# Matmul, GELU, matmul on one core: nine of the first twelve loads cast inside the transfer, and two banks for one turn

## The chip, the core and the metric

The kernel runs on one core of one Trainium2 chip. The metric is the device time of a run in microseconds (us), the median of three runs: 118.3 us for the kernel before (118.18 to 118.35). The profile is of one execution and spans 116.2 us from the first to the last instruction; TensorE's granted clock was 0.999 in it.

## The reference

```python
m, k, n, p = 1024, 1024, 2048, 1024          # a: m x k, b: k x n, c: n x p, all float32
h = np.matmul(a, b)
h = 0.5 * h * (1 + np.tanh(np.sqrt(2 / np.pi) * (h + 0.044715 * h ** 3)))
return np.matmul(h, c).astype(np.float32)
```

## The kernel before

The inputs lie in memory as float32. The kernel works with bf16 operands and with float32 sums of bf16 blocks, and its order is written out by hand: on each engine the instructions run in the order of the code.

**What is loaded, and how.** `a` is needed transposed. Its 1024 rows are cut into an upper and a lower half (h = 0, 1), its 1024 columns into four parts (q = 0 to 3) of 256. The first 512 columns of `b` are loaded by q too, two row tiles of 128 at a time. For each q there are three loads of 512 KB in float32: a's upper part, b's part, a's lower part. All twelve go on SyncE's queue (`load_a`, line 70, and `load_b`, line 74) into staging tiles `sta` and `stb`, still float32. The rest of `b` and the whole of `c`, fourteen transfers, go on GpSimd's queue (lines 89 to 95); those transfers cast to bf16 on the way, so each reads 1 MB and writes 512 KB. A copy of one column, `gate` (line 84), stands ahead of them on GpSimd: it waits for the load of a's lower part of q = 2, and so holds GpSimd's queue back.

A framework puts the waits in. On each of the two queues it uses eight completion counters in turn, so a transfer's issue waits until the one eight places ahead of it has landed.

**The first stage** (lines 214 to 294). For each part of `a`, `cast_a` casts the staged part to bf16 tiles `ab`, on VectorE (line 101) or ScalarE (line 99), or one half on each. `turn` (line 127) transposes it: in two halves (n = 0, 1), four transposes on TensorE into a PSUM bank (line 132) and a copy from the bank into `aT` by VectorE (line 133). `cast_b` casts b's rows on ScalarE (line 139). `block` issues matmuls that accumulate the products of the first row tiles of the hidden matrix (line 105), each 128x512 with 128 deep. The turns are split by `next(tn)`, so that matmuls stand between the two halves of a turn: a turn has one bank for both halves, and the second half's transposes wait for the copy of the first. `stir` (line 116) keeps TensorE at work before data is there. `zero.t1` and others (line 155) prepare sums of blocks on VectorE for the next stage.

One bank number matters for the change: the first turn of a's lower half, `turn(1, 0, 7, ab)` at line 225, uses bank 7, with two matmuls between its halves. Bank 6 is to hold `ps[1, 2]`, an accumulator that starts just after.

**The rest.** Three times a product of 2x2 blocks is computed with seven products instead of eight (class `Seven`, function `seven`, matmuls at line 197): `zero` and `one` for the rest of the hidden matrix, with b's other columns, and `two` for the second matmul with `c`. Each result tile of `two` is stored by SyncE (line 436), most as one transfer of 128x512.

Of the kernel before, what the change touches and what calls it, by code (L numbers as in the profile page):

```python
# [9 lines left out]
F32 = mybir.dt.float32  # L10
F32R = mybir.dt.float32r
BF16 = mybir.dt.bfloat16
# [7 lines left out]
def kernel(ctx, tc, a, b, c, out):  # L20
    nc = tc.nc
    M, K = a.shape
    _, N = b.shape
    _, P = c.shape
    H = 512
# [3 lines left out]
    av = a.rearrange("(mt p) k -> p mt k", p=128)  # L29
    bv = b.rearrange("(kt p) n -> p kt n", p=128)  # L30
# [9 lines left out]
    def slot(tag, shape, dt, name):  # L40
        return big.tile(shape, dt, name=name, tag=tag)

    def bank(i, shape=(128, H), dt=F32, name="ps"):
        return pp.tile(list(shape), dt, name=name, tag=f"bank{i}", padded_shape=None)

    def pieces(tag, bufs, shape, dt, name):
        return small.tile(shape, dt, name=name, tag=tag, bufs=bufs)
# [5 lines left out]
    gate = consts.tile([128, 1], F32, name="gate")  # L53
# [7 lines left out]
    b1 = slot("b1", [128, KT, 1024], BF16, "b1")  # L61
# [2 lines left out]

    KH = KT // 2
    stb = slot("x0", [128, KT, H], F32, "stb")
    sta = [slot(f"x{i}", [128, 2, 2, 4, 256], F32, "sta") for i in (1, 3)]

    def load_a(h, q):
        nc.sync.dma_start(out=sta[q // 2][:, h, q % 2],  # L70
                          in_=av[:, 4 * h:4 * h + 4, ds(q * 256, 256)])

    def load_b(q):
        nc.sync.dma_start(out=stb[:, 2 * q:2 * q + 2], in_=bv[:, 2 * q:2 * q + 2, 0:H])

    load_a(0, 0)
    load_b(0)
    load_a(1, 0)
    for q in range(1, 4):
        load_a(0, q)  # L80
        load_b(q)
        load_a(1, q)

    nc.gpsimd.tensor_copy(gate, sta[1][:, 1, 0, 3, 0:1])
    nc.scalar.activation(g, warm[:, 0:1], AF.Gelu_apprx_tanh)


    for k in range(0, KT, 4):
        nc.gpsimd.dma_start(out=b1[:, k:k + 4, H:], in_=bv[:, k:k + 4, ds(H, H)])
    for n in range(2):  # L90
        for k in range(0, KT, 4):
            nc.gpsimd.dma_start(out=b2[:, k:k + 4, ts(n, H)],
                                in_=bv[:, k:k + 4, ds(1024 + n * H, H)])
# [3 lines left out]
    def copy(eng, dst, src):  # L97
        if eng is nc.scalar:
            nc.scalar.activation(dst, src, AF.Copy)  # L99
        else:  # L100
            nc.vector.tensor_copy(dst, src)  # L101

    def mm1(p, t, h, ks):
        for k in ks:
            nc.tensor.matmul(p, b1[:, k, ts(t, 128)], aT[:, h, k],  # L105
                             start=(k == 0), stop=(k == KT - 1))
# [6 lines left out]
    def stir(*widths):  # L113

        for w in widths:
            nc.tensor.matmul(ps[0, 3][:, 0:w], warm[:, 0:128], warm[:, 0:w],  # L116
                             start=True, stop=True, skip_group_check=True)

    def cast_a(h, q, *engs):

        ab = pieces("ab", 2, [128, 4, 256], BF16, "ab")
        for i, eng in enumerate(engs):
            w = 256 // len(engs)
            copy(eng, ab[:, :, ts(i, w)], sta[q // 2][:, h, q % 2][:, :, ts(i, w)])
        return ab

    def turn(h, q, i, ab):

        pt = bank(i, (128, 2, H), BF16, "pt")
        for n in range(2):  # L130
            for m in range(4):
                nc.tensor.transpose(pt[:, n, ts(m, 128)], ab[:, m, ts(n, 128)], ident)  # L132
            nc.vector.tensor_copy(aT[:, h, 2 * q + n], pt[:, n])  # L133
            yield

    def cast_b(k, n=1):
        for i in range(n):
            r = ds(i * (H // n), H // n)
            nc.scalar.activation(b1[:, k, r], stb[:, k, r], AF.Copy)  # L139

    def block(h, tiles, ks):
        for k in ks:
            for t in tiles:
                mm1(ps[h, t], t, h, (k,))
# [62 lines left out]
    def quarters(b, c0, w):  # L207
        return [[b[:, 0:4, ds(c0, w)], b[:, 4:8, ds(c0, w)]],
                [b[:, 0:4, ds(c0 + w, w)], b[:, 4:8, ds(c0 + w, w)]]]

    zero = Seven(4, quarters(b1, H, 256), BB, [None] * 4, [None] * 4, 2)
    one = Seven(4, quarters(b2, 0, H), BB, [None] * 4, zero.t)

    stir(256, 256, 256, 256)
    tn = turn(0, 0, 4, cast_a(0, 0, nc.vector))
    next(tn)
    stir(256)
    next(tn)
    stir(128)
    cast_b(0, 2)  # L220
    cast_b(1)
    ab = cast_a(1, 0, nc.vector, nc.scalar)
    block(0, range(4), (0,))
    block(0, range(2), (1,))
    tn = turn(1, 0, 7, ab)
    next(tn)
    block(0, range(2, 4), (1,))
    next(tn)
    for t in range(3):
        ps[1, t] = bank(4 + t)  # L230
    zero.t[0], zero.t[1] = pair(2)
    zero.t1(4, 0)
    ab = cast_a(0, 1, nc.scalar, nc.scalar)
    block(1, range(3), (0,))
    tn = turn(0, 1, 7, ab)
    next(tn)
    block(1, range(3), (1,))
    next(tn)
    cast_b(2)
    cast_b(3)  # L240
    ab = cast_a(1, 1, nc.vector, nc.scalar)
    block(0, range(4), (2,))
    block(0, range(1), (3,))
    tn = turn(1, 1, 7, ab)
    next(tn)
    block(0, range(1, 4), (3,))
    next(tn)
    zero.t1(4, 1)
    ab = cast_a(0, 2, nc.scalar, nc.scalar)
    block(1, range(3), (2,))  # L250
    tn = turn(0, 2, 7, ab)
    next(tn)
    block(1, range(3), (3,))
    next(tn)
    cast_b(4)
    cast_b(5)
    ab = cast_a(1, 2, nc.vector, nc.scalar)
    block(0, range(4), (4,))
    block(0, range(1), (5,))
    tn = turn(1, 2, 7, ab)  # L260
    next(tn)
    block(0, range(1, 4), (5,))
    next(tn)
    zero.t1(4, 2)
    ab = cast_a(0, 3, nc.scalar, nc.scalar)
    block(1, range(3), (4,))
    tn = turn(0, 3, 7, ab)
    next(tn)
    block(1, range(3), (5,))
    next(tn)  # L270
    zero.t1(4, 3)
    cast_b(6)
    cast_b(7)
    ab = cast_a(1, 3, nc.scalar, nc.vector)
    block(0, range(4), (6, 7))
    zero.t2(2, 0)
    for t in range(4):
        gelu(t, 0, ps[0, t])
    ps[1, 3] = bank(7)
    mm1(ps[1, 3], 3, 1, range(2))  # L280
    tn = turn(1, 3, 0, ab)
    next(tn)
    mm1(ps[1, 3], 3, 1, range(2, 5))
    next(tn)
# [150 lines left out]
    def store(mt, q0, w, ot, eng=None):  # L435
        (eng or nc.sync).dma_start(out=out[ts(mt, 128), ds(q0, w)], in_=ot)

    def done2(i, l, j, p):
        if (i, l) == (1, 0):
            ot = pieces("o", 4, [128, H], F32, "ot")  # L440
            nc.vector.tensor_copy(ot, p)
            p = ot
        n = 2 if (i, l) == (0, 0) else 1
        for q in range(n):
            r = ds(q * (H // n), H // n)
            store(4 * i + j, l * H + q * (H // n), H // n, p[:, r])

    def between2(n):
# [12 lines left out]
        elif n == "P73":  # L461
            two.t4(two.t[1], 4)

    seven(two, done2, between2)


# [28 lines left out]
```

## Time and profile before

| | us |
|---|---|
| time, median of 3 | 118.3 |
| span of the profile | 116.2 |
| TensorE busy in the span | 111.7 |
| VectorE, ScalarE, GpSimd busy | 90.3, 59.3, 11.0 |
| from the first transposes (line 132) to the first matmul of line 197, by the chain | 4.99 to 24.95 |
| the 400 matmuls of line 197, by the chain | 88.03 |

How to read the profile: PE is TensorE's matmul side, PEld its weight load, DVE is VectorE, ACT ScalarE, POOL GpSimd, SP SyncE; POOLq and SPq are those engines' own instruction queues. A row of the timeline is the start, the duration, the engine, the line, the operation and its tiles, and in brackets how long the engine had been idle and what ended that. Ends of matmuls are modelled: a matmul of 512 columns is shown as 379 ns although the next one starts after 216, so starts are to be compared and not busy times. "The chain of waits" follows the execution back from its last instruction, at each step to what released it; each of its rows is a start, a length and what the time went to. Of the transfers the profile gives packets and bytes by queue: q1 holds SyncE's, q0 GpSimd's. The bytes of casting transfers are counted as they are written, in bf16, so 206 GB/s there means 412 GB/s read.

While the first stage runs, the transfers move 390 GB/s or so from 7 us on (391 between 10 and 13 us), and 298 between 2.9 and 5.8 us.

### The profile page before, as it was taken

The page shows a single profiled execution, that of the slowest core. Times are in us where ns is not written, and L with a number is a line of the kernel's source. Part 1 is how long each engine was busy: PE and PEld are TensorE (multiplying, and loading weights), DVE is VectorE, ACT ScalarE, POOL GpSimd, SP SyncE. Part 2 cuts the span into 40 slices and gives each one's busy share as a digit, 9 for nine tenths or more (in the row PEclk, how much of TensorE's full clock was granted, in tenths as well). Part 3 has the DMA queues.
Part 4 walks back from the last instruction along what each step waited for, and adds up shares of the span by engine and source line. Part 5 has one row for each costly group of instructions (what it writes and reads, how often), then busy time and mean ns, then how long its engine had stood idle before and what let it go on. Part 6 is the DMA issues. An engine that isn't in the chain of part 4 may idle for free.

```text
span 116.2 us, 1478 instructions
## 1 busy us (share of the span) xinstructions
PE 111.7 (96%) x540; PEld 76.9 (66%) x540; DVE 90.3 (78%) x107; ACT 59.3 (51%) x99; POOL 11.0 (9%) x21
## 2 busy tenths in 40 slices
PE   5999999999999999999999999999999999999980
PEld 4655555545777447888885444588888888888860
DVE  0336666889998999844699999999999986954770
ACT  5067668989269998066699329600034982000000
POOL 2000049623322000000000000000000000000000
PEclk9999999999999999999999999999999999999999
DMA  2999999999999999998000000070000002014993
GB/s 83 298 356 393 395 395 321 206 206 206 206 208 213 211 213 211 213 209 164 4 0 0 0 6 0 7 264 0 0 0 0 0 0 96 0 69 171 370 364 109
DMA packets 13542, 17.91 MB, mean 154 GB/s; under 512 B 736, under 2 KB 8928, under 8 KB 13536
## 3 DMA queue, kind: packets, MB, share of 16 engines
q0 software_dynamic: 5344, 7.34, 35.6%
q1 hardware_dynamic: 8192, 10.49, 25.2%
q8 instruction: 4, 0.07, 0.2%
q14 instruction: 2, 0.02, 0.0%
HBM read 20.97 MB, written 4.19 MB: 217 GB/s over the span
## 4 chain that ended last, share of the span: by engine, by line
PE 96%; DVE 1%; issue 0%
PE ps L197 76%; PE ps L105 12%; PE ps L116 4%; PE pt L132 4%; DVE aT L133 0%; DVE ot L382 0%; DVE warm L50 0%
## 5 line engine op out<-in xcount | busy, mean ns | idle before, releaser
L197 PE MATMUL ps<-x,s 128*128 128x512 f32 x128 | 29.6, 391 | 0.0
L197 PEld LDWEIGHTS ps<-x,s 128*128 128x128 f32 x128 | 24.0, 188 | 5.1
L197 PE MATMUL ps<-x,x 128*128 128x512 f32 x96 | 22.9, 394 | 0.0
L197 PEld LDWEIGHTS ps<-x,x 128*128 128x128 f32 x96 | 18.0, 188 | 3.9
L105 PE MATMUL ps<-aT,b 128*128 128x512 bf16 x64 | 16.3, 379 | 0.0
L305 ACT ACTIVATE v<-ps 128x512 f32<-128x512 f32 x10 | 6.0, 598 | 19.4 <-PE ps L197 19.4
L197 PE MATMUL ps<-c_sb,hT 128*128 128x512 bf16 (+1 forms) x72 | 14.2, 356 | 0.0
L197 PE MATMUL ps<-x 128*128 128x512 f32 x56 | 13.2, 393 | 0.0
L197 PEld LDWEIGHTS ps<-x 128*128 128x128 f32 x56 | 10.2, 188 | 2.7 <-ACT u L305 0.4
L133 DVE COPY aT<-pt 128x512 bf16<-128x512 bf16 x16 | 6.8, 424 | 6.4 <-PE pt L132 6.4
L197 PEld LDWEIGHTS <-hT 128*128 128x128 bf16 x72 | 6.9, 98 | 7.0 <-issue 0.5
L109 ACT ACTIVATE hT<-ot 128x512 bf16<-128x512 f32 x18 | 10.5, 625 | 1.5 <-DVE ot L310 1.3
L310 DVE TENSOR_TENSOR ot<-ps,v 128x512 f32<-128x512 f32 x10 | 6.7, 688 | 5.2 <-DMA out_dram<-ot 3.8
L197 PE MATMUL ps<-aT,b 128*128 128x512 bf16 x48 | 10.7, 379 | 0.0
L310 DVE TENSOR_TENSOR ot<-ps,u 128x512 f32<-128x512 f32 x10 | 6.7, 689 | 5.1 <-ACT u L305 5.1
L155 DVE TENSOR_TENSOR x<-c_sb 128x1024 fp32r<-128x1024 bf16 x8 | 9.2, 1221 | 0.0
L132 PEld LDWEIGHTS <-ab 128*128 128x128 bf16 x64 | 4.9, 102 | 5.5 <-DVE ab L101 1.9
L197 PEld LDWEIGHTS <-b 128*128 128x128 bf16 x48 | 4.6, 97 | 5.7 <-issue 0.3
L105 PEld LDWEIGHTS <-b 128*128 128x128 bf16 x64 | 5.5, 98 | 4.1 <-ACT b L139 0.5
L99 ACT ACTIVATE ab<-sta 128x512 bf16<-128x512 f32 x10 | 6.0, 625 | 3.3 <-DMA sta<-in_a_dram 3.3
L305 ACT ACTIVATE u<-ps 128x512 f32<-128x512 f32 x10 | 5.8, 596 | 3.4 <-PE ps L197 3.2
L109 ACT ACTIVATE hT<-ps 128x512 bf16<-128x512 f32 x14 | 7.3, 596 | 0.4 <-PE ps L105 0.3
(39 smaller groups left out, 115.6 us busy)
## 6 DMA issues: line engine op xcount, KB each, us to landing
sta<-in_a_dram SPq DMA_DIRECT2D x8, 512.0 KB, 8.4
c_sb<-in_c_dram POOLq DMA_DIRECT2D x8, 512.0 KB, 19.9
b<-in_b_dram POOLq DMA_DIRECT2D x6, 512.0 KB, 11.5
out_dram<-ot SPq DMA_DIRECT2D x12, 256.0 KB, 2.1
stb<-in_b_dram SPq DMA_DIRECT2D x4, 512.0 KB, 8.0
out_dram<-ot SPq DMA_DIRECT2D x8, 128.0 KB, 2.0
```

The costliest lines, as they stand in the source:

```text
L99: nc.scalar.activation(dst, src, AF.Copy)
L105: nc.tensor.matmul(p, b1[:, k, ts(t, 128)], aT[:, h, k], start=(k == 0), stop=(k == KT - 1))
L109: nc.scalar.activation(hT[h][:, t], p, AF.Gelu_apprx_tanh)
L116: nc.tensor.matmul(ps[0, 3][:, 0:w], warm[:, 0:128], warm[:, 0:w], start=True, stop=True, skip_group_check=True)
L132: nc.tensor.transpose(pt[:, n, ts(m, 128)], ab[:, m, ts(n, 128)], ident)
L133: nc.vector.tensor_copy(aT[:, h, 2 * q + n], pt[:, n])
L155: nc.vector.tensor_tensor(out=dst[:, r], in0=x[:, r], in1=y[:, r], op=op)
L197: nc.tensor.matmul(p[:, ds(c0, w)], l[:, k, ts(j, 128)], r[:, k, ds(c0, w)], start=(start and k == 0), stop=(k == self.kt - 1), skip_group ...
L305: nc.scalar.activation(st, p, AF.Copy)
L310: nc.vector.tensor_tensor(out=ot, in0=p, in1=st, op=ADD)
```

## The change

Only the first three loads stay on SyncE's queue: a's upper part, b's part and a's lower part of q = 0. The other nine go on GpSimd's queue, ahead of what it had, and are cast to bf16 inside the transfer: a's parts into a new tile `abq`, b's parts right into `b1`. So their casts on ScalarE and VectorE, and their waits for them, fall away. The copy `gate` that opens GpSimd's queue now waits for a's first load instead of its lower part of q = 2. With the staging no longer needed, the code for q = 1 and 2 becomes a loop; the order of the matmuls and turns in it is kept.

The first turn of a's lower half gets two banks, 7 and 6, one for each half, so that its eight transposes follow each other; the two matmuls that stood between the halves come after them.

In the last stage the first stored tile of the block (1, 1) goes out in two transfers of 128x256 instead of one. SyncE's queue has 24 transfers in all then.

```diff
-    sta = [slot(f"x{i}", [128, 2, 2, 4, 256], F32, "sta") for i in (1, 3)]
...
-    load_a(0, 0)
-    load_b(0)
-    load_a(1, 0)
-    for q in range(1, 4):
-        load_a(0, q)
-        load_b(q)
-        load_a(1, q)
-
-    nc.gpsimd.tensor_copy(gate, sta[1][:, 1, 0, 3, 0:1])
+    sta = slot("x1", [128, 4, 4, 256], F32, "sta")
+    abq = slot("x3", [128, 4, 2, 4, 256], BF16, "abq")
...
+    nc.sync.dma_start(out=sta[:, 0], in_=a_part(0, 0))
+    nc.sync.dma_start(out=stb[:, 0:2], in_=b_part(0))
+    nc.sync.dma_start(out=sta[:, 1], in_=a_part(1, 0))
+
+    nc.gpsimd.tensor_copy(gate, sta[:, 0, 3, 0:1])
...
+    def cast_load_a(h, q):
+        nc.gpsimd.dma_start(out=abq[:, q, h], in_=a_part(h, q))
+
+    def cast_load_b(q):
+        nc.gpsimd.dma_start(out=b1[:, 2 * q:2 * q + 2, 0:H], in_=b_part(q))
+
+    for q in range(1, 4):
+        cast_load_a(0, q)
+        cast_load_b(q)
+        cast_load_a(1, q)
...
     def turn(h, q, i, ab):
-        pt = bank(i, (128, 2, H), BF16, "pt")
+        banks = i if isinstance(i, tuple) else (i,)
+        pts = [bank(x, (128, 2, H), BF16, "pt") for x in banks]
         for n in range(2):
+            pt = pts[n % len(pts)]
...
-    ab = cast_a(1, 0, nc.vector, nc.scalar)
+    ab = cast_a(1, nc.vector, nc.scalar)
     block(0, range(4), (0,))
     block(0, range(2), (1,))
-    tn = turn(1, 0, 7, ab)
-    next(tn)
+    for _ in turn(1, 0, (7, 6), ab):
+        pass
     block(0, range(2, 4), (1,))
-    next(tn)
...
-    ab = cast_a(0, 1, nc.scalar, nc.scalar)
     block(1, range(3), (0,))
-    tn = turn(0, 1, 7, ab)
+    tn = turn(0, 1, 7, abq[:, 1, 0])
...
-    cast_b(2)
-    cast_b(3)
-    ab = cast_a(1, 1, nc.vector, nc.scalar)
...
-        n = 2 if (i, l) == (0, 0) else 1
+        n = 2 if (i, l) == (0, 0) or (i, l, j) == (1, 1, 0) else 1
```

More of the change, by code (lines that the diff above doesn't have):

```diff
@@ L66, with a_part, b_part @@
     stb = slot("x0", [128, KT, H], F32, "stb")
-    sta = [slot(f"x{i}", [128, 2, 2, 4, 256], F32, "sta") for i in (1, 3)]
[L69 to L74, printed above, removed]
-    load_a(0, 0)
-    load_b(0)
-    load_a(1, 0)
-    for q in range(1, 4):
-        load_a(0, q)
-        load_b(q)
-        load_a(1, q)
-    nc.gpsimd.tensor_copy(gate, sta[1][:, 1, 0, 3, 0:1])
-    nc.scalar.activation(g, warm[:, 0:1], AF.Gelu_apprx_tanh)
+    sta = slot("x1", [128, 4, 4, 256], F32, "sta")
+    abq = slot("x3", [128, 4, 2, 4, 256], BF16, "abq")
+    def a_part(h, q):
+        return av[:, 4 * h:4 * h + 4, ds(q * 256, 256)]
+    def b_part(q):
+        return bv[:, 2 * q:2 * q + 2, 0:H]
+    nc.sync.dma_start(out=sta[:, 0], in_=a_part(0, 0))
+    nc.sync.dma_start(out=stb[:, 0:2], in_=b_part(0))
+    nc.sync.dma_start(out=sta[:, 1], in_=a_part(1, 0))
+    nc.gpsimd.tensor_copy(gate, sta[:, 0, 3, 0:1])
+    nc.scalar.activation(g, warm[:, 0:1], AF.Gelu_apprx_tanh)
+    def cast_load_a(h, q):
+        nc.gpsimd.dma_start(out=abq[:, q, h], in_=a_part(h, q))
+    def cast_load_b(q):
+        nc.gpsimd.dma_start(out=b1[:, 2 * q:2 * q + 2, 0:H], in_=b_part(q))
+    for q in range(1, 4):
+        cast_load_a(0, q)
+        cast_load_b(q)
+        cast_load_a(1, q)
     for k in range(0, KT, 4):
@@ L117, in stir, with cast_a @@
                              start=True, stop=True, skip_group_check=True)
-    def cast_a(h, q, *engs):
+    def cast_a(h, *engs):
         ab = pieces("ab", 2, [128, 4, 256], BF16, "ab")
@@ L123, in cast_a @@
             w = 256 // len(engs)
-            copy(eng, ab[:, :, ts(i, w)], sta[q // 2][:, h, q % 2][:, :, ts(i, w)])
+            copy(eng, ab[:, :, ts(i, w)], sta[:, h][:, :, ts(i, w)])
         return ab
     def turn(h, q, i, ab):
-        pt = bank(i, (128, 2, H), BF16, "pt")
+        banks = i if isinstance(i, tuple) else (i,)
+        pts = [bank(x, (128, 2, H), BF16, "pt") for x in banks]
         for n in range(2):
+            pt = pts[n % len(pts)]
             for m in range(4):
@@ L214 @@
     stir(256, 256, 256, 256)
-    tn = turn(0, 0, 4, cast_a(0, 0, nc.vector))
+    tn = turn(0, 0, 4, cast_a(0, nc.vector))
     next(tn)
@@ L238 @@
     next(tn)
-    cast_b(2)
-    cast_b(3)
-    ab = cast_a(1, 1, nc.vector, nc.scalar)
[L242 to L270, printed above, removed]
+    for q in range(1, 3):
+        k = 2 * q
+        block(0, range(4), (k,))
+        block(0, range(1), (k + 1,))
+        tn = turn(1, q, 7, abq[:, q, 1])
+        next(tn)
+        block(0, range(1, 4), (k + 1,))
+        next(tn)
+        zero.t1(4, q)
+        block(1, range(3), (k,))
+        tn = turn(0, q + 1, 7, abq[:, q + 1, 0])
+        next(tn)
+        block(1, range(3), (k + 1,))
+        next(tn)
     zero.t1(4, 3)
-    cast_b(6)
-    cast_b(7)
-    ab = cast_a(1, 3, nc.scalar, nc.vector)
     block(0, range(4), (6, 7))
@@ L280 @@
     mm1(ps[1, 3], 3, 1, range(2))
-    tn = turn(1, 3, 0, ab)
+    tn = turn(1, 3, 0, abq[:, 3, 1])
     next(tn)
```

## The prediction

> **What bounds the kernel now.** I read the chain that ended last first: it says which engine sets the end, and where that engine is not the one.
>
> ```profile
> PE 96%; DVE 1%; issue 0%
> PE ps L197 76%; PE ps L105 12%; PE ps L116 4%; PE pt L132 4%; DVE aT L133 0%; DVE ot L382 0%; DVE warm L50 0%
> ```
>
> TensorE carries the end; line 197, the three Seven stages, is 76% of it and untouched. Only the first 25 us can move (lines 105, 132, 116). The same chain in order of time shows where TensorE is not the link there:
>
> ```profile
> 7.18 1.32 PE ps L105 x6
> 8.50 0.35 PE pt L132 x4
> 8.85 0.02 issue
> 8.88 0.44 DVE aT L133
> 9.31 0.04 issue
> 9.36 0.38 PE pt L132 x4
> 9.74 0.65 PE ps L105 x3
> 10.39 0.25 PE pt L132 x4
> ...
> 24.95 88.03 PE ps L197 x400
> ```
>
> From 9.36 to 24.95 there is no link but TensorE; the single break is VectorE's copy of the first lower turn's first half (8.88 to 9.31). Was TensorE really full after it? The timeline gives starts: matmuls follow each other by about 0.2155 us (three span 0.81 with a modelled 0.379 for the last), four transposes take about 0.22. A step of q is 14 matmuls and 16 transposes: 3.02 + 0.88 = 3.90 us. The turns begin at 8.44, 12.51 and 16.57, so it really takes 4.06 us; the 0.16 are waits at the changes, such as for the copy between the halves of a turn.
>
> The loads are as fast. TensorE's transposes follow a's lower loads, which VectorE and ScalarE begin to cast at 12.03, 16.07 and 20.09: 4.04 us per three loads. So TensorE and the transfers are level, and an arrival that slips shows in the end. That makes the queue's start decisive:
>
> ```profile
> 16.02 0.18 POOL L84 COPY gate<-sta 128x1 f32<-128x1 f32 x1 [14.72 <-DMA sta<-in_a_dram]
> 16.14 1.62 POOL L89 DMA_DIRECT2D b<-in_b_dram  x2
> ...
> 23.51 0.70 POOL L95 DMA_DIRECT2D c_sb<-in_c_dram  x1 [1.39 <-DMA b<-in_b_dram]
> 26.05 0.71 POOL L95 DMA_DIRECT2D c_sb<-in_c_dram  x1 [1.83 <-DMA b<-in_b_dram]
> ```
>
> The gate passes at 16.02, the first casting load is issued at 16.14, and GpSimd's ninth and tenth transfers wait for the first and second to land: 23.51 and 26.05. By the DMA counts for 18 to 19 us
>
> ```profile
> q1 hardware_dynamic: 367, 0.37, 104.9%
> q0 software_dynamic: 4, 0.00, 2.7%
> ```
>
> GpSimd's queue (q0) had moved four packets by 19.0. So its data starts about 2.8 us after the first issue; SyncE's queue (q1) drains at 19.3.
>
> **What the Trainium skill says.** (1) "DMA: Bandwidth & Descriptors", SWDGE vs HWDGE vs iDMA: a cast inside a transfer must be issued from GpSimd, and all issuers share the same 16 engines. The trace agrees: 206 GB/s written in bf16 is 412 GB/s read, against 395 on SyncE's queue. (2) Same page, Latency and other measured facts: first byte after about 1 us from GpSimd. Here it is 2.8 us, behind a busy queue; the measurement is my value, 1 us plus the first issue's 0.87 us my lower bound. (3) Same page, Queues, rings and completion order: an engine takes its queues in turn, packet by packet. The two queues overlap here for some 0.3 us only, so the trace hardly tests it. (4) "PSUM — Partial Sum Buffer", Terms: TensorE and VectorE must not be in one bank at once. The trace agrees: the second four transposes start at 9.36, after the copy's end at 9.31.
>
> **The change, part by part.** *Two banks for the first lower turn.* It runs all 8 transposes, then two matmuls, then the block of three. Transposes 8.44 to 8.66 and, as ScalarE's half of the cast ends at 8.59, on to 8.88; two matmuls (0.43) to 9.31; the three matmuls need the first copy (8.88 to 9.31), so they start at about 9.36. Before they start at 9.57: **0.21 us gained**. VectorE's line 155 subtraction also moves up behind the second copy (10.12 to 9.74 at best), so the next copy no longer waits for it; this takes up to 0.06 off the transposes at 11.19: **0.27 in all**. Bank 6 is only wanted at the third of the three matmuls, near 9.8, with the second copy over at 9.74.
>
> *Casts removed.* ScalarE loses six line 139 casts and nine of the ten of line 99 (some 0.6 us each), VectorE three of line 101 (0.43). None is a link of the chain after 9.36, so **nothing** directly; but an arrival is now used at once, 0.4 to 1.2 us earlier than a cast one.
>
> *Nine loads to GpSimd's queue.* The gate moves to a's first load, whose cast starts at 4.24. So first issue about 4.37, data from 4.37 + 2.8 = 7.2. SyncE's three loads need 1.57 MB; its counts reach 1.58 MB at 7.25. So one queue starts where the other ends, as at 19 us, and the third load should land at 7.96 as before.
> A 512 KB b load (2 KB read per packet) takes half of the 2.54 us between 23.51 and 26.05, 1.27 us. An a load reads 1 KB and writes 512 bytes per packet, which no transfer before does. Lower bound: c's packets (4 KB read, 212 GB/s written, 2.47 us per transfer, 154 ns per packet and engine) and b's (2 KB, 79 ns) lie on a line with some 5 ns fixed, so 42 ns for 1 KB and 32 x 42 = 1.34 us per load. Upper bound: such a packet costs as much as a 2 KB one, 2.54 us. I take 1.34: twice the packet size nearly doubled its time. A step is then 1.34 + 1.27 + 1.34 = 3.95 us, under TensorE's 4.06.
> From the last byte to the waiter: SyncE's last load drains by 19.3 and is used at 20.09, 0.8 us. The first GpSimd load reaches its 0.52 MB at 21.9 and is used at 23.51, 1.6 us. I take 1.1, as a load of half the size lets the engines drift apart less, and keep 0.8 and 1.6.
> Arrivals: a upper 7.2 + 1.34 + 1.1 = 9.6, b 10.9, a lower 12.3. TensorE, 0.21 to 0.27 ahead of before, wants them at 10.05, 11.1 and 12.25. In time, the last to within 0.05; later steps gain 0.11 each.
>
> *Queued behind.* On GpSimd the b1, b2 and c loads now wait behind nine more. In bytes nothing is added: the stream ends 0.3 us earlier or so. VectorE's first use of b1's upper half (26.05) feeds a product at 28.05 and has 0.7 us to spare, c more than 4 us. GpSimd's eight first issues, at 0.8 us, end near 10.8; the ninth's wait for the first landing (9.6) is over by then. **Nothing.**
>
> *One store split in two.* It lies near 95 us, 18 us before the last store, and the ending's order is as before. SyncE issues one more in slack it waits out: **nothing**.
>
> Sum: 118.3 - 0.27 = **118.0 us**.
>
> **The rivals.** *The stream is late (0.25).* With the measured 1.6 us the arrivals are 10.1, 11.4 and 12.8; the last is wanted at 12.25 and came into use at 12.51 before. The wait for the casts is replaced by one for a longer landing, once; the later steps catch up but TensorE can't. That gives 118.3 + 0.3 = 118.6. For it: 1.6 is the only measured value. Against it: that transfer was twice as large and started beside a draining queue.
> *A collision (0.13).* With 0.87 + 1 us the data starts at 6.3, while SyncE has 0.28 MB to move. Taken in turn, its third load ends up to 0.7 us later (0.28 MB at 395 GB/s), 0.35 if spare bandwidth takes half: it moved only 290 to 360 GB/s then. 118.3 + 0.35 - 0.21 = 118.4. Against it: at 16.14 the same start left SyncE's loads at their pace.
> *Earlier first loads (0.14).* From 4.0 to 5.5 the DMA moved only 184 to 262 GB/s. If the loads queued behind cause this, b's first load (used at 6.56) is up to 0.6 us sooner, and the matmuls with it, until the stream's 9.6 limits: 117.7. Against it: the queue is served in order.
> *Packets of 512 bytes are slow (0.08).* A step takes 2.54 + 1.27 + 2.54 = 6.35 us; the last a load arrives at 7.2 + 3 x 6.35 + 1.1 = 27.4, wanted at 21.7: 118.3 + 5.7 = 124.0.
>
> **How the numbers follow.** The forecast, in time, has 0.40: 118.0. Below 118.06 lie most of it (0.37) and the earlier loads (0.13): faster 0.50. Within 0.2% lie its rest and parts of the collision and the late stream: 0.18. Slower: 0.32, from the late stream (0.19), the slow packets (0.08), a strong collision (0.05). The range goes from 117.6 to 118.8; it leaves out the slow packets, the tail of a still later stream and a little of the early case, under 0.2.
>
> **What would show it.** In the chain of waits the link by VectorE near 8.9 is gone, the three matmuls after the first lower turn start near 9.36, and the stage before line 197's 400 matmuls ends at 24.7. The first GpSimd packets appear at 7.2. Transposes of abq that wait for their load at 10 or 12.3 mean the late stream; SyncE's third load later than 7.96, the collision; a step of more than 4.1 us in GpSimd's loads, slow packets. Wrong would be a forecast whose 400 matmuls take another length than 88.0 us, for I move nothing there.

## The result, and the profile after

The change makes the kernel slower. Where two or more runs were compared, the ratio to the kernel before stands with its 95% interval.

| | before | after |
|---|---|---|
| time, median, us | 118.32 | 119.29 (119.18 to 119.42) |
| ratio | | 1.0084 [1.0066, 1.0101] |
| span of the profiled execution, us | 116.2 | 117.6 |
| start of the 400 matmuls of the Seven stages | 24.95 | 26.36 |
| their length | 88.03 | 87.99 |

The profiled execution of after lost 1.4 us, the median of its runs 1.0: how much is lost differs from one execution to the next.

First the chain that ended last, by engine and by line, for after:

```profile
PE 85%; DMA 9%; POOL 2%; DVE 0%; issue 0%
PE ps L205 75%; PE ps L111 8%; DMA abq<-in_a_dram 6%; DMA sta<-in_a_dram 3%; PE pt L140 2%; POOL abq L85 1%; POOL gate L80 1%; POOL b L88 1%; DVE ot L367 0%
```

TensorE had 96% of the chain before and has 85% now; 9% are transfers, and GpSimd, which was not in it, has 2%. In order of time (start, length, what):

```profile
0.74 3.49 DMA sta<-in_a_dram
...
4.29 0.70 POOL gate L80
4.99 0.81 POOL abq L85
5.80 0.68 POOL b L88
6.49 7.44 DMA abq<-in_a_dram
...
13.97 0.40 PE pt L140 x4
...
26.36 87.99 PE ps L205 x400
```

Until 13.97 the chain is a's first load, the gate, GpSimd's issues, and then one transfer: `abq`, a's lower part of q = 1. From its transposes on there is only TensorE, as before. So all the loss lies ahead of 13.97, where before stood at 12.51; the 1.46 us shrink to 1.41 at the 400 matmuls and stay. The timeline (start, duration, engine, line, operation, count, in brackets the idle time and what ended it) shows where TensorE waited. First three rows of before, then after:

```profile
9.57 0.81 PE L105 MATMUL ps<-aT,b 128*128 128x512 bf16 x3
...
11.41 1.24 PE L105 MATMUL ps<-aT,b 128*128 128x512 bf16 x5
...
12.51 0.40 PE L132 MATMUL pt<-ident,ab 128*128 128x128 bf16 x4
```

```profile
9.05 1.26 PE L111 MATMUL ps<-aT,b 128*128 128x512 bf16 x5
...
10.15 0.39 PE L140 MATMUL pt<-ident,abq 128*128 128x128 bf16 x4
...
12.54 1.25 PE L111 MATMUL ps<-aT,b 128*128 128x512 bf16 x5 [1.10 <-DMA b<-in_b_dram]
...
13.97 0.40 PE L140 MATMUL pt<-ident,abq 128*128 128x128 bf16 x4 [0.18 <-DMA abq<-in_a_dram]
```

The first casting load, a's upper part, is used at 10.15 with no wait. The second, b's part of q = 1, is waited for until 12.54; in before, these matmuls began at 11.41. The third adds some 0.3 us. What the transfers did meanwhile is in the stretches of half a microsecond. The columns are busy time and count of TensorE, its weight load, VectorE, ScalarE and GpSimd, then TensorE's clock, the DMA share and, last, GB/s as written:

```profile
7.50:8.00 0.50, 0.50 (x4) 0.18 (x2) 0.00 (x0) 0.46 (x1) 0.50 (x2) 1.00 1.38 188
8.50:9.00 0.50, 0.50 (x9) 0.41 (x8) 0.04 (x1) 0.24 (x1) 0.50 (x2) 1.00 1.00 147
9.50:10.00 0.50, 0.50 (x4) 0.25 (x3) 0.50 (x2) 0.00 (x0) 0.50 (x1) 1.00 0.93 113
10.00:10.50 0.50, 0.50 (x7) 0.36 (x6) 0.39 (x1) 0.00 (x0) 0.50 (x2) 1.00 0.69 85
12.50:13.00 0.50, 0.46 (x3) 0.23 (x4) 0.00 (x0) 0.00 (x0) 0.21 (x1) 1.00 1.46 196
```

From 12.5 to 19.0 us the casting transfers write 194 to 207 GB/s, about 200 in the mean; I call this full pace. From 8.5 to 11.0 the five stretches have 147, 136, 113, 85 and 109: a mean of 118, so 0.205 MB are missing, or 1.03 us of full pace; the three to 12.5 (154, 174, 184) lack 0.22 us more. This **dip**, 1.25 us in all, is most of the 1.46 us. The DMA share falls along with the rate, from 1.38 at 188 GB/s to 0.69 at 85 (a share above 1 means that an engine has more than one packet under way): the single packet took little longer, but the engines had, in the mean, only half as many in hand. The experiments ask what makes the dip.

### The profile page after: what moved, and what is told of

It reads as the page before. It is cut to its first block, busy times and chain, and to the rows that moved or that the text cites. A ratio compares the mean times of both kernels' runs of the same rounds, so it can differ in the third digit from the quotient of the medians.

```text
span 117.6 us, 1451 instructions
## 1 busy us (share of the span) xinstructions
PE 111.4 (95%) x540; PEld 76.7 (65%) x540; DVE 89.2 (76%) x104; ACT 50.6 (43%) x84; POOL 18.2 (15%) x30
## 4 chain that ended last, share of the span: by engine, by line
PE 85%; DMA 9%; POOL 2%; DVE 0%; issue 0%
PE ps L205 75%; PE ps L111 8%; DMA abq<-in_a_dram 6%; DMA sta<-in_a_dram 3%; PE pt L140 2%; POOL abq L85 1%; POOL gate L80 1%; POOL b L88 1%; DVE ot L367 0%
## 5 line engine op out<-in xcount | busy, mean ns | idle before, releaser
L290 ACT ACTIVATE v<-ps 128x512 f32<-128x512 f32 x10 | 6.0, 599 | 19.5 <-PE ps L205 19.5
L205 PE MATMUL ps<-x 128*128 128x512 f32 x56 | 13.2, 392 | 0.0
L101 POOL DMA_DIRECT2D c_sb<-in_c_dram x8 | 5.6, 702 | 12.6 <-DMA b<-in_b_dram 11.9
L163 DVE TENSOR_TENSOR x<-b 128x1024 fp32r<-128x1024 bf16 (+1 forms) x4 | 7.0, 1751 | 0.3 <-issue 0.3
```

Source lines behind the costliest of these rows:

```text
L101: nc.gpsimd.dma_start(out=c_sb[:, t:t + 2], in_=cv[:, t:t + 2])
L163: nc.vector.tensor_tensor(out=dst[:, r], in0=x[:, r], in1=y[:, r], op=op)
L205: nc.tensor.matmul(p[:, ds(c0, w)], l[:, k, ts(j, 128)], r[:, k, ds(c0, w)], start=(start and k == 0), stop=(k == self.kt - 1), skip_group ...
L290: nc.scalar.activation(st, p, AF.Copy)
```

## The experiments

The expectations name causes of the dip as they were thought of before each run. All kernels are changes of after unless said otherwise. In diffs, "+" and "-" are against that parent.

**1. Does the other half of the change do its part? Before, with only the two banks.**

```diff
-        pt = bank(i, (128, 2, H), BF16, "pt")
+        pts = [bank(x, (128, 2, H), BF16, "pt") for x in banks]
...
+    for _ in turn(1, 0, (7, 6), ab):
```

> The kernel before with one edit: two banks for the first lower turn; all loads stay on SyncE's queue. The prediction's first term says 0.2 to 0.27 us are gained, so 118.05 to 118.1. Rival: the stage is paced by the loads and their casts, so that what is gained at 9.4 us is waited away at the next cast (12.5 us): 118.3, no change. In the trace: the start of the turn that stood at 12.51 tells, 12.25 against 12.5.

118.24 us against 118.22, ratio 0.9999 [0.9985, 1.0012]: no gain. The timeline of this kernel:

```profile
8.90 1.26 PE L105 MATMUL ps<-aT,b 128*128 128x512 bf16 x5
...
9.70 1.15 ACT L99 ACTIVATE ab<-sta 128x512 bf16<-128x512 f32 x2 [1.12 <-DVE aT L135]
...
10.39 0.40 PE L134 MATMUL pt<-ident,ab 128*128 128x128 bf16 x4 [0.23 <-ACT ab L99]
```

The third of the five matmuls starts at 8.90 + 2 x 0.2155 = 9.33, against 9.57 in before: the 0.24 us are there. But ScalarE's next cast of `ab` starts at 9.70, and the next turn's transposes at 10.39 instead of 10.26. The view names VectorE's copies as what ended the cast's wait, since they end last, at 9.63. They can't be what it needs: in the kernel of experiment 13 the same cast starts while the copies are under way,

```profile
8.88 0.76 DVE L143 COPY aT<-pt 128x512 bf16<-128x512 bf16 x2 [0.49 <-PE pt L142]
...
9.48 1.15 ACT L107 ACTIVATE ab<-sta 128x512 bf16<-128x512 f32 x2 [0.89 <-DMA sta<-in_a_dram]
```

and there, as in before (9.44), its load is named. The cast waits for its load, which in this execution came some 0.27 us later than in the profiled one of before, as the loads behind it did (cast at 12.30 instead of 12.03). Loads at before's times would not have let the gain through either: the casts at 12.03 there can't start before their load has landed, and the transposes at 12.51 follow them. The saved wait has turned into one for the loads, as the rival had it.

**2. Does VectorE's cast hold the gate? ScalarE casts a's first part instead.**

```diff
-    tn = turn(0, 0, 4, cast_a(0, nc.vector))
+    tn = turn(0, 0, 4, cast_a(0, nc.scalar))
```

> The changed kernel, but a's first part is cast by ScalarE instead of VectorE. In the changed kernel the gate's copy on GpSimd took 0.70 us, just as long as VectorE's cast beside it, against 0.18 before. Theory 'lock': VectorE's cast holds the gate up; then the copy takes about 0.2 us here, GpSimd's first load is issued near 4.45 instead of 4.93, and the stream and the end come some 0.5 us sooner: 118.8. Rival 'the gate is just slow there': 0.70 again and 119.3. The cast itself takes 1.1 us on ScalarE instead of 0.7, which delays the first turn to 5.4 us but not the first matmuls, which wait for b at 7.2.

In after the copy `gate` of one element per partition took 0.70 us, from 4.29 to 4.99, next to VectorE's cast from 4.26 to 4.95. The timeline of GpSimd in this kernel:

```profile
4.28 0.18 POOL L80 COPY gate<-sta 128x1 f32<-128x1 f32 x1 [2.98 <-DMA sta<-in_a_dram]
4.40 0.87 POOL L85 DMA_DIRECT2D abq<-in_a_dram  x1
```

0.18 us, and the first issue at 4.40 instead of 4.93: the cast was the cause. It agrees with the Trainium skill, "SBUF — State Buffer", Who interferes with whom: a VectorE cast that takes the port pair shared with GpSimd shuts GpSimd out for the whole instruction. Yet the time is 119.77 us, 1.0137 [1.0107, 1.0167]. The dip is deeper (78 to 99 GB/s from 8.0 to 10.5) and b's part came in use at 13.51. Half a microsecond of earlier issue isn't the cure.

**3. Is it the load, or its place? b's part of q = 1 after a's lower part.**

```diff
     for q in range(1, 4):
         cast_load_a(0, q)
-        cast_load_b(q)
+        if q > 1:
+            cast_load_b(q)
         cast_load_a(1, q)
+        if q == 1:
+            cast_load_b(q)
```

> The changed kernel, but on GpSimd's queue b's part of q = 1 stands behind a's lower part instead of ahead of it. In the changed kernel that queue moved only 85 to 150 GB/s from 8.5 to 11.3 us, against 200 before and after, while b's part and a's lower part were in hand. Theory 'time': something at that time starves the queue, so the dip stays at 8.5 to 11.3 us and now stretches a's lower part. Theory 'rows': b's rows are slow to read the first time, as b's first part is on SyncE's queue (4.0 to 5.5 us, also in the kernel before); then the dip moves by the 1.3 us of one load, to 9.9 and later. TensorE waits for b at the same place in either case, so the time is 119.3 to 120.5.

One run, 122.39 us. The stretches have 118 to 165 GB/s from 7 to 10 us, 85 from 10.0 to 10.5 and 109 at 12, and b came in use at 14.31. Neither theory fits: slow stretches moved with b, but a's loads ahead of it were below full pace too. The time holds more than the loads' delay, for TensorE's clock was 0.50 from 14.5 to 17.5 us in this execution.

**4. Do VectorE's PSUM copies disturb GpSimd? They go to ScalarE for three turns.**

```diff
-            nc.vector.tensor_copy(aT[:, h, 2 * q + n], pt[:, n])
+            copy(nc.scalar if (h, q) in ((1, 0), (0, 1), (1, 1)) else nc.vector,
+                 aT[:, h, 2 * q + n], pt[:, n])
```

> The changed kernel, but the copies out of the banks for the turns (1,0), (0,1) and (1,1) are done by ScalarE instead of VectorE. Theory 'lock': VectorE's copies of bf16 and GpSimd's writing of descriptors shut each other out, and that starves the queue from 8.5 to 11.3 us; then the dip goes, b's part of q = 1 lands near 11.2 instead of 12.5, and the time falls by about 1 us to 118.3. Rival: the dip has another cause and stays; then the time is 119.3, or up to 0.2 more, as ScalarE's copy of 512 elements takes 0.6 us and VectorE's 0.42.

120.06 us, 1.0182 [1.015, 1.0213], and the dip is there (76 to 119 GB/s from 8.5 to 11.0). The copies aren't needed for it.

**5. and 6. Do the rows that b's part reads matter?** In one kernel it reads the rows of q = 0 again, in the other rows of `c`; their sums are of other data.

```diff
-        cast_load_b(q)
+        cast_load_b(q) if q > 1 else nc.gpsimd.dma_start(out=b1[:, 2:4, 0:H], in_=b_part(0))
```
```diff
-        cast_load_b(q)
+        cast_load_b(q) if q > 1 else nc.gpsimd.dma_start(out=b1[:, 2:4, 0:H], in_=cv[:, 2:4, 0:H])
```

> The changed kernel, but b's part of q = 1 on GpSimd's queue reads the rows of b's part of q = 0 once more instead of its own, so this part of the product is not the reference's; everything else is as it was. Theory 'rows': rows of b that are read for the first time, by a queue that has only just started, come slowly; then these rows, read 5 us earlier, come at full pace: no dip from 8.5 to 11.3 us, that load lands near 11.3, and the time is about 118.0 to 118.3. Rival 'time' or 'queue start': the dip does not ask which rows they are; then GpSimd's queue again moves 85 to 150 GB/s, the load lands at 12 to 13.5 and the time stays at 119 to 120.

> The changed kernel, but b's part of q = 1 on GpSimd's queue is read from c (256 rows of the same 2 KB, 4 KB apart instead of b's 8 KB), so this part of the product is not the reference's. Theory 'in step on far rows': the engines collide since b's rows lie 8 KB apart; then the dip from 8.5 to 11.3 us is gone or half as deep, the load lands by 11.7 and the time is 118.2 to 118.7. Rival: packets of 2 KB read collide whatever their distance; then it lands at 12 to 13.5 and the time stays at 119 to 120.

One run each, 119.05 and 119.99 us. Both have a dip, to 107 and 95 GB/s between 10.0 and 10.5, and b is used at 12.14 and 13.24. Neither the first touch of b's rows nor their distance is needed for the dip.

**7. Does GpSimd's issuing disturb its own transfers? It stops after q = 1's loads until b's part has landed.**

```diff
+        if q == 1:
+            nc.gpsimd.tensor_copy(gate, b1[:, 2, 0:1])
```

> The changed kernel with a second gate: after the three loads of q = 1, GpSimd waits for b's part of q = 1 to land before it issues more. Theory 'issue': GpSimd is writing descriptors from 4.9 to 11.6 us without a pause, and the engines that read them or move the data are held up by that; then the dip is gone once the third issue is over (7.3 us), and b's part lands near 11.3. Rival 'memory': packets of b wait for memory, whatever GpSimd does; then the dip stays, and b's part lands at 12 to 13.5. In both cases the queue stands still afterwards for some 2 us, until the next loads come, so the time is 120 to 122.

One run, 123.72 us. GpSimd issued nothing from 7.7 to 13.2 us, and still the transfers moved 125 and 120 GB/s between 10 and 11 us; b was used at 12.69. The issuing isn't needed for the dip. (TensorE's clock fell to 0.50 here too, from 20 to 22 us, so that the time says little.)

**8. b's part of q = 1 stays on SyncE's queue, as its fourth load.**

```diff
+    nc.sync.dma_start(out=stb[:, 2:4], in_=b_part(1))
...
-        cast_load_b(q)
+        if q > 1:
+            cast_load_b(q)
...
+    cast_b(2)
+    cast_b(3)
```

> The changed kernel, but b's part of q = 1 is the fourth load on SyncE's queue and is cast by ScalarE; the other eight stay on GpSimd's. Theory 'rows' or 'memory' on GpSimd's queue alone: SyncE's queue, which in the kernel before read the same rows at full pace, brings them by 9.5 to 10.5 us, with its cast done by 11.7, and then a's lower part, by 12, holds nobody: 118.2 to 118.4. Rival: the two queues in turn slow each other, a's upper part of q = 1 lands after 10.5, or a's lower part is late in its place: 119 or more.

119.08 us, 1.0074 [1.0057, 1.009]. There is no dip: from 9.5 us on GpSimd's queue moves 0.10 MB in each half microsecond. But its packets start only near 8.3 us, over 3 us after the issue at 5.06, while SyncE's queue is busy until 9.6; a's upper part is used at 11.39, 1.1 us later than in before (10.26). In this execution, the slowest of the four, 0.75 us of that were there earlier: b's first part was used at 7.34 instead of 6.56, and the first lower turn began at 9.19 instead of 8.44. The wait for a's upper part itself is 0.48 us. One loss is exchanged for another.

**9. The hand-over one step later: six loads on SyncE's queue, the gate on its third.**

```diff
+    nc.sync.dma_start(out=sta[:, 2], in_=a_part(0, 1))
+    nc.sync.dma_start(out=stb[:, 2:4], in_=b_part(1))
+    nc.sync.dma_start(out=sta[:, 3], in_=a_part(1, 1))
...
-    nc.gpsimd.tensor_copy(gate, sta[:, 0, 3, 0:1])
+    nc.gpsimd.tensor_copy(gate, sta[:, 1, 3, 0:1])
```

> Six loads on SyncE's queue instead of three (those of q = 0 and q = 1, cast by ScalarE and VectorE as in the kernel before), the gate opened by the third, and six cast inside GpSimd's transfers. Theory: the loss is all in the start of GpSimd's queue (first data 2 us after the issue, then slow packets); here this lies beside SyncE's loads of q = 1 and the loads of q = 2 have 1.5 us to spare, so the stage runs as before, 118.0 to 118.3. Rival: a dip follows the start of GpSimd's queue wherever it is and slows SyncE's last loads too: 118.8 or more.

119.15 us, 1.0083 [1.0067, 1.0099], as much as after. The stretches of this kernel:

```profile
13.00:13.50 0.50, 0.50 (x5) 0.21 (x3) 0.39 (x1) 0.00 (x0) 0.50 (x2) 1.00 1.16 163
13.50:14.00 0.50, 0.50 (x7) 0.32 (x5) 0.04 (x1) 0.00 (x0) 0.50 (x2) 1.00 1.02 133
```

The dip is there, shallower and some 4 us later, and over by 16; a's lower part of q = 2 is used at 17.36 instead of 16.57. The loss follows the hand-over.

**10. and 11. An earlier start: the gate taken away, with three and with six loads on SyncE's queue.**

```diff
-    nc.gpsimd.tensor_copy(gate, sta[:, 0, 3, 0:1])
```

> The changed kernel without the gate: GpSimd issues its first load at about 1.3 us, so its queue is full before SyncE's drains. Theory 'in step': the 16 DMA engines, when a queue starts on all of them at once, run in step and then collide on b's next part; once apart they stay apart, so a stream that never runs dry is not slowed. Then, if SyncE's loads go first, there is no dip between 8.5 and 11.3 us, b's part of q = 1 lands near 11.2 and the time is 118.0 to 118.4. Rival 'collision': the two queues share the engines from 3.3 us on, SyncE's third load lands at 9 us or later instead of 8.1, and the time is 118.8 to 120.

> Six loads on SyncE's queue and six on GpSimd's, without a gate. Theory 'in step': GpSimd's queue is full when SyncE's drains at about 11.3 us, so nothing runs dry; if SyncE's loads go first, the loads of q = 2 come in time and the time is 118.0 to 118.3, against 119.15 with the gate. Rival 'collision': GpSimd's packets come in between from 3.3 us on and delay SyncE's loads of q = 0 and q = 1: 118.8 to 120.

With three: 119.21 us, 1.0066 [1.0041, 1.0091]. GpSimd issues from 1.42, its packets come from 6.1 us on, and there is no dip (196 to 235 GB/s from 8.0 to 10.5). The chain of waits and the timeline of this kernel:

```profile
1.76 7.59 DMA sta<-in_a_dram
```
```profile
9.37 0.43 DVE L106 CAST ab<-sta 128x512 bf16<-128x512 f32 x1 [2.26 <-DMA sta<-in_a_dram]
```

Now SyncE's third load is late: cast at 9.37 instead of 7.96. From 7.0 to 8.5 us GpSimd's queue moves 0.17 MB as written and SyncE's 0.18; they share the engines. With six loads it is plainer: 124.4 us, 1.0529 [1.0483, 1.0575], with SyncE's a lower part of q = 1 cast at 18.02 instead of 12.03, since the loads that are wanted later take their share for 10 us. (In the profiled execution, of 125.6 us, TensorE's clock was 0.50 for a while as well; an execution at full clock took 124.3.) The Trainium skill, "DMA: Bandwidth & Descriptors", Queues, rings and completion order, says that an engine takes its queues in turn, packet by packet; these runs agree: from 7.0 to 9.5 us the two queues of the six-load kernel moved 431 and 430 packets.

**12. Is it GpSimd's queue or the cast at all? Before, with a pause in SyncE's queue.** a's upper part of q = 2 is loaded over the lower one of q = 1, which has to be cast first. No product changes.

```diff
+    def place(h, q):
+        return sta[0][:, 1, 1] if (h, q) == (0, 2) else sta[q // 2][:, h, q % 2]
...
-        nc.sync.dma_start(out=sta[q // 2][:, h, q % 2],
+        nc.sync.dma_start(out=place(h, q),
```

> The kernel before, all loads on SyncE's queue, but a's upper part of q = 2 is loaded over a's lower part of q = 1 and so waits until that has landed (both then hold the same data, which is not the reference's). The queue runs dry at about 12 us and starts again on all engines at once some 1.5 us later. Theory 'in step': b's part of q = 2, the second load after the pause, then takes 1.7 us or more from the landing ahead of it (by the middle one of the 16 engines) instead of the 1.29 it takes in the kernel before, and its packets' times show a dip, though neither GpSimd nor a cast is in it. Rival 'GpSimd': the dip belongs to GpSimd's queue or to the cast, and b's part takes 1.3 us. The time is not of interest; the pause adds 2 to 4 us.

One run, 121.7 us. Its stretches (full pace is about 390 GB/s here, as nothing is cast on the way):

```profile
12.00:12.50 0.50, 0.50 (x3) 0.20 (x2) 0.20 (x1) 0.10 (x1) 0.00 (x0) 1.00 0.00 0
...
14.50:15.00 0.50, 0.00 (x0) 0.00 (x0) 0.00 (x0) 0.00 (x0) 0.00 (x0) 1.00 1.04 369
...
15.50:16.00 0.50, 0.00 (x0) 0.00 (x0) 0.20 (x1) 0.20 (x1) 0.00 (x0) 1.00 0.85 217
16.00:16.50 0.50, 0.22 (x4) 0.22 (x5) 0.22 (x1) 0.50 (x2) 0.00 (x0) 1.00 0.85 225
```

The queue is empty at 12, back at 369 GB/s by 14.5, and then falls to some 220 while b's part, the second load after the pause, is moved: 2.0 us for what takes 1.3 to 1.4 when the queue doesn't pause. So a stretch of half pace some 2 us after a fresh start can come without GpSimd's queue and without the cast. The slow stretches between 4.0 and 5.5 us, at the second load of the kernel (184 to 262 GB/s in before, 197 to 313 in after), fit this. But it isn't the dip over again. Here the share falls only from 1.04 to 0.85 where the rate falls from 369 to 217, so the packets took longer; in after the share halved with the rate. Whether the two have one cause is open, and with it whether GpSimd's queue has a part in after's dip.

**13. and 14. Can the hand-over be free of both? SyncE keeps a's upper part of q = 1 too (four loads), or also b's part (five); the gate stays.**

```diff
+    nc.sync.dma_start(out=sta[:, 2], in_=a_part(0, 1))
...
-        cast_load_a(0, q)
+        if q > 1:
+            cast_load_a(0, q)
...
+    ab = cast_a(0, 1, nc.scalar, nc.scalar)
```
```diff
+    nc.sync.dma_start(out=sta[:, 2], in_=a_part(0, 1))
+    nc.sync.dma_start(out=stb[:, 2:4], in_=b_part(1))
...
-        cast_load_a(0, q)
-        cast_load_b(q)
+        if q > 1:
+            cast_load_a(0, q)
+            cast_load_b(q)
```

> After, but a's upper part of q = 1 stays on SyncE's queue as its fourth load, still float32, and ScalarE casts it; the other eight stay on GpSimd's queue behind the same gate. Theory (GpSimd's queue begins afresh, and b's first load on it is slow for that): SyncE's queue now has work until about 9.3 us, so GpSimd's data, from 7 us on, starts beside it. If a queue that starts beside a busy one does not go slow, b of q = 1 lands near 11 as it is the first of its queue, a's lower part by 12.5, and the time is 118.0 to 118.5. Rival (the start behind a busy queue is late, as with b on SyncE's queue, where GpSimd's first packets came 3.1 us after the issue): first packets at 8.2 or later, b lands at 11.5 to 12.5, a's lower part after 13, 118.8 to 119.4. Second rival (the dip follows b's first load on GpSimd's queue wherever it stands): b takes over 1.8 us from its first packets and the time is 119.2 or more.

> After, but a's upper part and b's part of q = 1 stay on SyncE's queue, as its fourth and fifth loads, with their casts on ScalarE; GpSimd's queue begins with a's lower part of q = 1, wanted at 12.25. Theory (only a fresh start and the b load near it cost): SyncE's loads land at 9.4 and 10.7 as in the kernel before, a's lower part lands by 12.3 if GpSimd's first packets come by 10.7; the restart then falls on b of q = 2, wanted near 15.2: 118.1 to 118.6 if the slack there covers it. Rival (each hand-over from SyncE's to GpSimd's queue costs 0.7 us or more wherever it falls): like six loads on SyncE, 119.0 to 119.4, with a first late use at 12.9 or later.

Four: 118.74 us, 1.0044 [1.0025, 1.0064], the least loss of all kernels that move loads. The stretches that had 113 and 85 GB/s in after:

```profile
9.50:10.00 0.50, 0.50 (x4) 0.10 (x1) 0.50 (x2) 0.50 (x1) 0.50 (x1) 1.00 1.18 175
10.00:10.50 0.50, 0.50 (x6) 0.34 (x6) 0.24 (x1) 0.50 (x2) 0.50 (x2) 1.00 1.38 192
```

The dip is nearly gone, and with it half of after's loss (0.44% against 0.84%). What is left goes with a late hand-over: GpSimd's first packets come at 8.25, 3.3 us after their issue at 4.91 (in after 1.6), b is used at 11.63 and a's lower part at 12.97, against 11.41 and 12.51 in before. In 5 of 17 executions this kernel took 118.2 to 118.4 us, as long as before; in the others it lost. With five loads: 119.09 us, 1.0068 [1.0038, 1.0098]. GpSimd's packets come beside SyncE's fifth load from 9.2 on (4.3 us after the issue); the load, shared, lands at 11.54, its cast on ScalarE is back on the chain, and the matmuls start at 12.23. In both, the rival (a start behind a busy queue is late) came nearer than the theory.

**15. Is it the width of b's reads? b's part of q = 1 in two transfers that read 1 KB at a time.**

```diff
-        cast_load_b(q)
+        if q == 1:
+            for w in range(2):
+                nc.gpsimd.dma_start(out=b1[:, 2:4, ts(w, 256)], in_=bv[:, 2:4, ts(w, 256)])
+        else:
+            cast_load_b(q)
```

> After, but b's part of q = 1 comes on GpSimd's queue as two transfers of 256 columns, each reading 1 KB per row instead of 2 KB; the other loads are as in after. Theory (engines that start together fall over each other in b's 2 KB reads, which a's 1 KB reads did not): the dip between 8 and 10.5 us is gone or under half, b of q = 1 lands near 11.2, the time is 118.3 to 118.8. Rival (the width of b's reads has no part in it: any load that comes second after a fresh start is slow): the dip stays, b lands at 12 to 12.7, 119.1 to 119.8; two more instructions on GpSimd's queue cost at most 0.8 us of issue, which lies ahead of the data from the third transfer on and is not on the path.

119.73 us, 1.0115 [1.01, 1.0129]. The stretches of this kernel:

```profile
7.50:8.00 0.50, 0.50 (x4) 0.11 (x4) 0.43 (x1) 0.50 (x1) 0.50 (x1) 1.00 0.50 56
...
11.00:11.50 0.50, 0.50 (x7) 0.19 (x4) 0.21 (x1) 0.00 (x0) 0.50 (x2) 1.00 0.57 50
```

Two dips, one already in a's first load and one from 9.5 to 12.5, both deeper than after's. So b's read of 2 KB isn't needed, and a's loads can fall into a dip too.

**What is shown and what isn't.** Shown: in after a stretch of half pace follows the start of GpSimd's queue near 7 us, and it makes most of the loss; it moves with that start (9), and it goes where SyncE keeps one or two loads more (8, 13, 14) or the gate is away (10). It came also with the copies on ScalarE, with other rows, with narrower reads and with GpSimd not issuing: none of these is needed for it.

It would be natural to say that the dip goes when SyncE still has work as GpSimd's queue starts, but the traces don't bear that out: in after both queues have packets from 6.5 to 7.7 us, in experiment 13 from 8.25 to 9.0 only. What does go with the depth is the time from GpSimd's first issue to its first packet. It is 1.6 to 2.0 us in after and its deep relatives (2 to 7 and 15; lowest stretch after 8 us 50 to 109 GB/s), 2.3 in experiment 9 (133), 2.75 in before at 19 us (186, hardly a dip), and 3.2 or more in 8, 10, 11, 13 and 14 (175 and above). No experiment varies this time alone, so it is an order and not a cause. The plainest reading would be that too few loads had been issued; against it speaks experiment 7, whose loads had been issued over 2 us before its 120 GB/s.

Not shown: what leaves the engines with fewer packets, and why the depth differs between executions. The theory "in step" foretold the half pace of experiment 12, but no run tests the mechanism itself. No version beat the kernel before.

## Why the prediction was wrong

The forecast was 118.0 us and the range 117.6 to 118.8; 119.3 lies outside, on the other side of before.

- **The step that failed** is "So one queue starts where the other ends, as at 19 us", with the full pace taken from there, and in a small part "I take 1.1" for the time from the last byte to the waiter. The arrivals of b and of a's lower part, forecast as 10.9 and 12.3, came in use at 12.54 and 13.97, the second 1.67 us late. At full pace from 7.2 the three loads, 0.79 MB as written, would have been moved by 11.15; they were at 12.5. So about 1.4 us of the 1.67 are pace, and the dip alone is 1.25. From 12.5 to the use it took 1.4 us, 0.3 more than forecast: a load of half the size came little sooner than the 1.6 us read off the larger one. The price of a load was right: the later loads of 512 KB free GpSimd's next issue each 1.28 to 1.42 us (12.79, 14.21, and so on), against 1.27 for b and 1.34 for a. But from 8.5 to 12.5 us that price didn't hold. What makes the dip stays open.
- **"As at 19 us".** There GpSimd's first packet came 2.75 us after the issue and SyncE's last one ended at 19.6, not at 19.3, so that the queues overlapped for 0.75 us and not 0.3; and 190 and 186 GB/s from 19.5 to 20.5 are a slight dip. In after the wait was 1.6 us. The one hand-over that was looked at happened to be a mild one.
- **The gate.** "First issue about 4.37" was 4.93. The row at 16.02, 0.18 us, had no VectorE cast ahead of it; the gate at 4.29 had one, from 4.26 to 4.95 (experiment 2). The latency was over-sized by more: the first packets came 1.6 us after the issue instead of 2.8, and the bulk from 7.0 on, so that the data's start, forecast as 7.2, was about right by luck: two errors cancelled.
- **Two banks.** Of "0.21 us gained" 0.09 were there in after: the third of the five matmuls from 9.05 starts at 9.48 instead of 9.57, for a's lower part of q = 0 was cast at 8.11 instead of 7.96. The further 0.06 put the transposes at 11.05 instead of 11.19, 0.14 ahead, and then b's wait took it all. Alone in before it gained nothing, as TensorE then waits at the next turns for the loads and their casts (experiment 1).
- **The rivals.** The late stream had the right form, a wait for `abq` and for b once, with the later steps unable to catch up. It gave 118.6, since it took a longer landing for its cause and 0.3 us for its size. Those 0.3 us are there; the dip is four times that. The collision's mechanism was shown by experiments 10 and 11, but no cost of it shows in after: the third load was cast 0.15 us later than in before, and so was the second (6.71 against 6.56), ahead of all but six of GpSimd's packets. Slow packets of 512 bytes fell: GpSimd's loads kept a step of 4.0 us. Nor did b's first load come earlier.
- **Right:** casts removed, issues queued behind, and the store split in two cost or gain nothing that shows; the 400 matmuls took 87.99 us against 88.03.

The range failed since every case in it took the full pace of a stream that was already running.

## What to carry to other kernels

When TensorE and the loads are level, a load moved to another queue is paid for at the hand-over, not by its bytes: look at the first two or three transfers after the change in stretches of half a microsecond, at the rate and at the engines' share together. One hand-over that went well in a trace is no promise for another with a shorter time from issue to first packet. Starting the new queue earlier has its price too, since it then takes its share from the loads that are wanted first. A cheap copy that opens a queue belongs where VectorE isn't in a cast at that moment. A wait removed ahead of a cast counts as gained only once the load that the cast needs has been followed; and the engine that a view names as the end of a wait may only have been the last to end.

## What the runs showed of the hardware that was not expected

- After the start of GpSimd's queue the 16 engines fell from about 200 GB/s (written, cast) to 50 to 120 for 1 to 3 us, with their share falling alike; after a pause of SyncE's queue they fell from 369 to 217 without a cast, with packets that took longer.
- GpSimd's first packets came 1.6 us after the first issue at 4.93, but 3.3 and 4.3 us after issues at 4.91 and 4.94 with one and two more loads on SyncE's queue, and 4.7 us after one at 1.42.
- A copy of one element per partition on GpSimd took 0.70 us beside a VectorE cast of 0.69 us, 0.44 beside one of 0.43 (experiment 9), and 0.18 without one.
